# Stick-breaking heads: the causal mask as POOL selects in SBUF in place of a mask matmul into PSUM

## The chip, the cores and the metric

The kernel runs on one core of a Trainium2 chip. The metric is the device time of one execution in microseconds (us). The core's engines are named as the profile names them: PE (TensorE, with PEld for its weight loads), DVE (VectorE), ACT (ScalarE), POOL (GpSimd) and SP (which only issues DMAs here). Each engine takes its own instructions strictly in the order in which they stand in its queue; semaphores tie the engines together.

## What is computed

One decoder layer on 512 tokens of width 2048: a joint input projection, two groups of attention heads side by side, an output projection, a SwiGLU feed-forward part and a last RMSNorm, all in float32. The change touches the first group alone, 16 heads of causal stick-breaking attention with 64 dimensions each. Cut to what matters:

```python
z = jnp.einsum('bqhd,bkhd->bhqk', qf[:, q0:kend], kf[:, :kend])
causal = s < t
log_beta = jax.nn.log_sigmoid(z)
log_one_minus = jnp.where(causal, jax.nn.log_sigmoid(-z), 0.0)
survive = lax.cumsum(log_one_minus, axis=3, reverse=True) - log_one_minus
weights = jnp.where(causal, jnp.exp(log_beta + survive), 0.0)
outs.append(jnp.einsum('bhqk,bkhd->bqhd', weights, vf[:, :kend]))
```

So a key s counts for a query t only where s < t, in two places: in the sum of the logarithms and in the weights.

## The kernel before, in words

Float32 products are made of three passes over operands that are split into a high part (fp32r) and the rest: high by high, high by low, low by high. The long matrix products (input projection, output projection, feed-forward) keep PE fed throughout, and the attention is woven into them.

The stick-breaking part works on blocks. Head h has four key blocks i of 128 keys, taken in the order 3, 2, 1, 0. Scores are held with keys on the partitions and queries on the columns, so block i needs the queries from i*128 on: 128, 256, 384 and 512 columns for i = 3, 2, 1, 0. The 128 columns at the left of a block are its diagonal square, the only place where the mask cuts. There are 64 blocks in all. In what follows **A** is a head of odd number and **B** the even one behind it, and A2 is block 2 of head A. Before (line numbers of the profile) a block runs through these steps:

- scores (`sb_qk`): two matmuls on PE (L600, L601) into a PSUM bank z, then the mask matmul (L602): identity times a bf16 tile that holds -1e30 where the mask cuts, added to the diagonal square of z;
- softplus (`sb_log`, `sb_sp`): ACT takes abs, exp and ln (L614, L615, L616), DVE makes max(z, 0) + that (L623, tile e), ACT copies it to fp32r (L624, tile h) and DVE takes the rest (`sb_lo`, L629, tile l). At masked places z is about -1e30, so softplus is 0;
- running sums over blocks (`sb_acc`) for i = 2 and 1 on POOL: L641 to L651, ten instructions in a head, of which the five of i = 1 (L641, L642, L649, L651, L650) follow each other closely;
- sum (`sb_sum`): two or four matmuls onto z (L661 to L664) that subtract the sums of softplus;
- weights (`sb_w`, `sb_wsplit`): ACT takes exp of z (L669, tile e again; 0 at masked places), DVE casts it (L674) and takes the rest (L675);
- values (`sb_av`): two matmuls (L684, L685) into the head's output bank; behind block 0 ACT and DVE add its two halves (L511, L513), and behind each pair of heads the squares are added up by ACT and POOL (L520, L521).

The loop over the 64 blocks works on several blocks at a time: the logarithms of block j, the sum and weights of j-1, the values of j-2. Between these it pulls steps of the input projection (L390 to L392, with L219 on ACT and L220 on DVE splitting their weights), so that PE has other work while the chain goes over ACT, DVE and POOL. Every second head also gets the q and k of two later heads staged (L488, L491, L497 to L500, L506, L507). The queue order of each engine is not the order of the code: a scheduler sets it when the program is built, except for instructions that are pinned to program order, which are none of those in the list above.

In the constants at the start, DVE makes `identb` and `maskb` and POOL sets and selects `scm`.

Of the kernel before, what the change touches and what calls it, by code (L numbers as in the profile page):

```python
# [8 lines left out]
F32 = mybir.dt.float32  # L9
F32R = mybir.dt.float32r  # L10
BF16 = mybir.dt.bfloat16
I32 = mybir.dt.int32
AF = mybir.ActivationFunctionType
ALU = mybir.AluOpType
AX = mybir.AxisListType

P = 128
# [8 lines left out]
IN_COLS = 4608  # L26
C_SBQ, C_SBK, C_SBV, C_SWQ, C_SWK, C_SWV = 0, 1024, 2048, 3072, 4096, 4352
EPS = 1e-5
NEG = -1.0e30
FAR = 1.0e32  # L30
QSCALE = HD ** -0.5
GF = 4
# [5 lines left out]
def tile_hymba(ctx: ExitStack, tc: tile.TileContext, x, ln_mix, w_in, sb_norm, swa_norm,  # L38
# [6 lines left out]
    const = ctx.enter_context(tc.tile_pool(name="const", bufs=1))  # L45
# [29 lines left out]
    def pz():  # L75
        return zs[1].tile([P, 512], F32, tag="z", name="z", bufs=4)
# [17 lines left out]
    def tmp(dt=F32, name="t"):  # L94
        return phase[1].tile([P, 512], dt, tag="t", name=name, bufs=phase[2])
# [9 lines left out]
    mm = nc.tensor.matmul  # L105
    V = nc.vector
    A = nc.scalar
    G = nc.gpsimd
# [15 lines left out]
    ident = const.tile([P, P], F32, name="ident")  # L124
    make_identity(nc, ident)
    ones = const.tile([P, P], F32, name="ones")
    G.memset(ones, 1.0)
    identb = const.tile([P, P], BF16, name="identb")
    neg1 = const.tile([P, P], F32R, name="neg1")
    negu = const.tile([P, P], F32R, name="negu")  # L130
    maskb = const.tile([P, P], BF16, name="maskb")
    sink = const.tile([P, 16], F32, name="sink")

    def constants():
        V.tensor_copy(out=identb, in_=ident)
        V.tensor_scalar(out=neg1, in0=ones, scalar1=-1.0, scalar2=None, op0=ALU.mult)
        scr = tmp(F32, "scr")[:, 0:P]
        G.affine_select(out=scr, in_=ones, pattern=[[-1, P]], compare_op=ALU.is_ge, fill=0.0,
                        base=0, channel_multiplier=1)
        V.tensor_scalar(out=negu, in0=scr, scalar1=-1.0, scalar2=None, op0=ALU.mult)  # L140
        scm = tmp(F32, "scm")[:, 0:P]
        G.memset(scm, 0.0)
        G.affine_select(out=scm, in_=scm, pattern=[[1, P]], compare_op=ALU.is_gt, fill=NEG,
                        base=0, channel_multiplier=-1)
        V.tensor_copy(out=maskb, in_=scm)
        nc.gpsimd.dma_start(out=sink, in_=sinks[0].partition_broadcast(P))

    gcol = const.tile([P, 48], F32, name="gcol")
# [330 lines left out]
    for c in (3, 4):  # L479
        while pos[0] < c - 3 or pos[1] < 3:  # L480
            step()
        load_x(c)
    turn2 = gain_cols([ln_ffn[0], sb_norm[0], swa_norm[0]], 16)
    defer(8, constants)
    defer(16, turn2)

# [101 lines left out]
    def geom(i):  # L588
        c0 = i * P if i < 3 else 256
        return S - i * P, c0, i * P - c0, S - c0  # L590

    def sb_qk(h, i):
        H = heads[h]
        n, c0, off, W = geom(i)
        B = Head()
        H.blk[i] = B
        zb = pz()
        B.zb, B.z = zb, zb[:, off:W]
        kb = H.ks[:, i * P:(i + 1) * P]
        mm(zb[:, 0:W], lhsT=kb, rhs=H.q1[:, c0:S], start=True, stop=False)  # L600
        mm(zb[:, 0:W], lhsT=kb, rhs=H.q2[:, c0:S], start=False, stop=True)  # L601
        mm(zb[:, off:off + P], lhsT=identb, rhs=maskb, start=False, stop=True, skip_group_check=True)  # L602

    def sb_log(h, i):
        H = heads[h]
# [12 lines left out]
    def sb_sp(h, i):  # L618
        H = heads[h]
        B = H.blk[i]  # L620
        n, c0, off, W = geom(i)
        e = B.e
        V.scalar_tensor_tensor(out=e, in0=B.z, scalar=0.0, in1=e, op0=ALU.max, op1=ALU.add)  # L623
        A.activation(out=B.h[:, off:W], in_=e, func=AF.Copy)  # L624
    def sb_lo(h, i):
        H = heads[h]
        B = H.blk[i]
        n, c0, off, W = geom(i)
        V.tensor_tensor(out=B.l[:, off:W], in0=B.e, in1=f(B.h)[:, off:W], op=ALU.subtract)  # L629
        if i == 3:  # L630
            H.acc[2] = (B.h, B.l, 256)
# [34 lines left out]
    def sb_w(h, i):  # L666
        B = heads[h].blk[i]
        n, c0, off, W = geom(i)
        A.activation(out=B.e, in_=B.z, func=AF.Exp)  # L669

    def sb_wsplit(h, i):
        B = heads[h].blk[i]
        n, c0, off, W = geom(i)
        V.tensor_copy(out=B.wh[:, off:W], in_=B.e)  # L674
        V.tensor_tensor(out=B.wl[:, off:W], in0=B.e, in1=f(B.wh)[:, off:W], op=ALU.subtract)  # L675
# [24 lines left out]
    sb_begin(0)  # L700
    pull(4000.0, sb_mark)
    at(sb_qk, 0)
    for j in range(NJ + 2):
        if j + 3 < NJ and jobs[j + 3][1] == 3:
            sb_begin(jobs[j + 3][0])
        at(sb_log, j)
        at(sb_qk, j + 1)
        pull(SBFILL / 3, sb_mark)
        at(sb_sum, j - 1)
        at(sb_w, j - 1)  # L710
        at(sb_sp, j)
        at(sb_acc, j)
        pull(SBFILL / 3, sb_mark)
        at(sb_av, j - 2)
        at(sb_wsplit, j - 1)
        at(sb_lo, j)
        pull(SBFILL / 3, sb_mark)
# [10 lines left out]
                    base=P, channel_multiplier=1)  # L728
    G.affine_select(out=dist, in_=dist, pattern=[[1, 256]], compare_op=ALU.is_ge, fill=FAR,
                    base=-1, channel_multiplier=-1)  # L730
# [929 lines left out]
```

## Time and profile before

| what | value |
|---|---|
| time, median of 3 runs | 2018.02 us (2017.5 to 2018.03) |
| span of the profiled execution, first to last instruction | 2015.3 us |
| median run less that span | 2.7 us |
| stick-breaking part, first to last mask matmul | 129.1 to 382.5 us |
| granted TensorE clock, mean | 0.998 |

The span is what the trace covers; the time of a run has a little on top of it, for what lies ahead of the first instruction and behind the last. That the granted clock is at 0.998 means that PE's speed was not reduced at any point that matters here. A row of the groups view reads: line, engine, operation, output tile <- input tiles, output size <- input size, count | busy us, mean ns of one | idle time of the engine just before, and who ended it. A row of the timeline reads: start us, duration us, engine, line, operation.

### The profile page before, as it was taken

What the parts mean: (1) busy time and instruction counts of PE and PEld (TensorE: products, weight loads), DVE (VectorE), ACT (ScalarE), POOL (GpSimd) and SP (SyncE); (2) the same over time, 40 slices, a digit from 0 to 9 for tenths busy, and PEclk for the clock granted to TensorE, in tenths of its full rate; (3) what the DMA queues carried; (4) which work ended last, traced back from release to release, by engine and by line L of the source; (5) the groups of instructions that cost most, each with busy time, mean ns of one, the idle gap of its engine ahead of it and who ended that gap; (6) DMA issues with size and microseconds to landing.
All of it is one profiled execution on the core that took longest, in us unless ns stands there. A gap on an engine that the chain in (4) does not pass through costs nothing.

```text
span 2015.3 us, 29246 instructions
## 1 busy us (share of the span) xinstructions
PE 2002.2 (99%) x10412; PEld 1707.3 (85%) x10412; DVE 1453.2 (72%) x1968; ACT 1455.7 (72%) x2009; POOL 1031.9 (51%) x562
## 2 busy tenths in 40 slices
PE   9999999999999999999999999999999999999998
PEld 8888888898788888888888888888888888888886
DVE  4358888768963777777777777777777867767767
ACT  5347777657842477777777777777777788788787
POOL 0014444300100066766667666666766778878883
PEclk9999999999999999999999999999999999999999
DMA  5332222222343354453544535444454743533523
GB/s 192 92 93 65 64 66 71 63 84 67 103 147 114 120 157 125 111 141 101 136 116 120 137 101 140 112 124 132 104 141 106 266 157 111 180 128 106 175 86 115
DMA packets 286369, 240.23 MB, mean 119 GB/s; under 512 B 11024, under 2 KB 237392, under 8 KB 283792
## 3 DMA queue, kind: packets, MB, share of 16 engines
q1 hardware_dynamic: 285552, 235.71, 39.6%
q8 instruction: 82, 1.34, 0.3%
q0 software_dynamic: 288, 1.32, 0.2%
q10 hardware_dynamic: 384, 1.34, 0.2%
q14 instruction: 63, 0.52, 0.1%
HBM read 218.40 MB, written 19.92 MB: 118 GB/s over the span
## 4 chain that ended last, share of the span: by engine, by line
PE 97%; DVE 1%; ACT 1%; issue 0%; DVEq 0%; POOL 0%; ACTq 0%; POOLq 0%
PE o L118 34%; PE m L118 28%; PE m L390 4%; PE m L391 4%; PE m L392 4%; PE m L359 2%; PE m L358 2%; PE m L360 2%; PE o L360 2%; PE o L359 2%; PE o L358 2%; PE z L118 1%; PE z L359 1%; PE z L360 1%; PE z L358 1%; PE z L853 1%
## 5 line engine op out<-in xcount | busy, mean ns | idle before, releaser
L118 POOL TENSOR_TENSOR t<-raw,t 128x1024 f32<-128x1024 f32 x107 | 272.6, 2548 | 277.5 <-ACT hp L118 263.3
L118 DVE TENSOR_TENSOR wlo<-t,hp 128x1024 fp32r<-128x1024 f32 x235 | 286.5, 1219 | 172.3 <-PE o L118 107.5
L118 ACT ACTIVATE whi<-t 128x1024 fp32r<-128x1024 f32 x235 | 249.3, 1061 | 123.1 <-PE o L118 74.7
L118 PE MATMUL o<-hca,whi 128*128 128x512 f32 x880 | 307.5, 391 | 0.0
L118 POOL TENSOR_TENSOR t<-raw,raw 128x1024 f32<-128x1024 f32 x106 | 275.3, 2601 | 16.0 <-issue 10.3
L118 DVE TENSOR_TENSOR wlo<-raw,hp 128x1024 fp32r<-128x1024 f32 x175 | 213.6, 1221 | 81.3 <-issue 50.5
L118 ACT ACTIVATE whi<-raw 128x1024 fp32r<-128x1024 f32 (+1 forms) x177 | 187.1, 1057 | 99.8 <-PE m L118 72.0
L118 PE MATMUL o<-hca,wlo 128*128 128x256 f32 x880 | 244.0, 280 | 0.0
L118 ACT ACTIVATE hp<-t 128x1024 fp32r<-128x1024 f32 x235 | 236.9, 1008 | 0.0
L220 DVE TENSOR_TENSOR wlo<-raw,whi 128x1024 fp32r<-128x1024 f32 x103 | 126.5, 1228 | 137.7 <-ACT whi L219 135.0
L219 ACT ACTIVATE whi<-raw 128x1024 fp32r<-128x1024 f32 x103 | 108.7, 1056 | 152.2 <-PE o L360 75.4
L118 PEld LDWEIGHTS o<-hca,whi 128*128 128x128 f32 x880 | 164.2, 187 | 35.8
L118 PE MATMUL m<-hca,whi 128*128 128x512 f32 x528 | 186.3, 392 | 1.1 <-DVE hca L118 1.1
L118 ACT ACTIVATE hp<-raw 128x1024 fp32r<-128x1024 f32 x179 | 180.8, 1010 | 3.1 <-DVE wlo L118 2.2
L118 PEld LDWEIGHTS o<-hca,wlo 128*128 128x128 f32 x880 | 165.6, 189 | 0.4
L390 PE MATMUL m<-hhi,whi 128*128 128x512 f32 x384 | 156.3, 407 | 0.0
L391 PE MATMUL m<-hlo,whi 128*128 128x512 f32 x384 | 150.5, 392 | 0.0
L392 PE MATMUL m<-hhi,wlo 128*128 128x512 f32 x384 | 150.4, 392 | 0.0
L118 PE MATMUL m<-whi,dca 128*128 128x512 f32 x592 | 146.9, 389 | 0.0
L118 PE MATMUL o<-whi,dca 128*128 128x512 f32 x592 | 146.8, 389 | 0.0
L118 PE MATMUL m<-hca,wlo 128*128 128x256 f32 x528 | 146.3, 280 | 0.0
L118 PEld LDWEIGHTS o<-whi,dca 128*128 128x128 f32 x592 | 111.1, 188 | 23.1
(351 smaller groups left out, 5143.6 us busy)
## 6 DMA issues: line engine op xcount, KB each, us to landing
raw<-in_w_gate_up_dram SPq DMA_DIRECT2D x348, 256.0 KB, 5.2
raw<-in_w_down_dram SPq DMA_DIRECT2D x68, 512.0 KB, 4.8
raw<-in_w_in_dram SPq DMA_DIRECT2D x39, 512.0 KB, 3.5
raw<-in_w_in_dram SPq DMA_DIRECT2D x66, 256.0 KB, 3.3
raw<-in_w_out_dram SPq DMA_DIRECT2D x32, 512.0 KB, 3.8
aT<-w SPq DMA_DIRECT2D x44, 256.0 KB, 3.5
xd<-aT SPq DMA_DIRECT2D x10, 1024.0 KB, 7.1
rx<-in_w_down_dram SPq DMA_DIRECT2D x20, 512.0 KB, 5.7
```

What stands on the lines that cost most here:

```text
L118: return lambda *a, **k: tc.keep_in_program_order(fn(*a, **k))
L219: A.activation(out=hi, in_=raw, func=AF.Copy)
L220: V.tensor_tensor(out=lo, in0=raw, in1=f(hi), op=ALU.subtract)
L358: mm(o, lhsT=lh[:, sl], rhs=hi[:, j, :], start=first, stop=False, skip_group_check=halves)
L359: mm(o, lhsT=lh[:, sl], rhs=lo[:, j, :], start=False, stop=False, skip_group_check=halves)
L360: mm(o, lhsT=ll[:, sl], rhs=hi[:, j, :], start=False, stop=(k == nslab * a - 1), skip_group_check=halves)
L390: mm(o, lhsT=wh, rhs=xh, start=(k == 0), stop=False)
L391: mm(o, lhsT=wh, rhs=xl, start=False, stop=False)
L392: mm(o, lhsT=wl, rhs=xh, start=False, stop=(k == KT - 1))
L853: nc.tensor.transpose(out=pb[:, hh * P:(hh + 1) * P], in_=B.s[hh // 2][:, hh % 2, j * P:(j + 1) * P], identity=ident)
```

## The change

The mask matmul goes, with the tiles `identb` and `maskb` and the instructions that made them. In its place POOL runs an affine select on the diagonal square of tile e, in place, which writes 0 where the mask cuts: once behind the softplus (L623) and once behind the exp of the weights (L669). In the changed file the select is L595, and the lines behind the constants have other numbers: L617 is L623 of before, L624 is L629, L670 is L674, L671 is L675, L504 is L513, L211 is L220, L489, L490, L491 and L498 are L498, L499, L500 and L507, and on POOL L636, L637, L644, L646, L645 and L512 are L641, L642, L649, L651, L650 and L521.

```diff
-    identb = const.tile([P, P], BF16, name="identb")
-    maskb = const.tile([P, P], BF16, name="maskb")
...
-        V.tensor_copy(out=identb, in_=ident)
...
-        G.memset(scm, 0.0)
-        G.affine_select(out=scm, in_=scm, pattern=[[1, P]], compare_op=ALU.is_gt, fill=NEG,
-                        base=0, channel_multiplier=-1)
-        V.tensor_copy(out=maskb, in_=scm)
...
         mm(zb[:, 0:W], lhsT=kb, rhs=H.q2[:, c0:S], start=False, stop=True)
-        mm(zb[:, off:off + P], lhsT=identb, rhs=maskb, start=False, stop=True, skip_group_check=True)
+
+    def causal(e):
+        G.affine_select(out=e[:, 0:P], in_=e[:, 0:P], pattern=[[1, P]], compare_op=ALU.is_gt, fill=0.0,
+                        base=0, channel_multiplier=-1)
...
         V.scalar_tensor_tensor(out=e, in0=B.z, scalar=0.0, in1=e, op0=ALU.max, op1=ALU.add)
+        causal(e)
         A.activation(out=B.h[:, off:W], in_=e, func=AF.Copy)
...
         A.activation(out=B.e, in_=B.z, func=AF.Exp)
+        causal(B.e)
```

PE's queue stays as it was but for the missing mask matmuls and one step of the first head. The queues of DVE, ACT and POOL are put in another order by the scheduler. The names in the rows below carry the tile's number: e2 is the tile of a block 2, and so on.

POOL before, from the running sums of head 4 (a B) to the squares of the heads 2 and 3:

```order
L642 CAST ah2_1830<-e2_1809 128x128
L646 COPY af_1834<-e2_1809 128x128
L641 TENSOR_TENSOR ah2_1830<-e3_1771,e2_1809 128x128
L645 TENSOR_TENSOR af_1834<-e3_1771,e2_1809 128x128
L647 TENSOR_TENSOR al2_1831<-af_1834,ah2_1830 128x256
L641 TENSOR_TENSOR ah1_1885<-af_1834,e1_1862 128x256
L642 CAST ah1_1885<-e1_1862 128x128
L649 TENSOR_TENSOR af_1834<-af_1834,e1_1862 128x256
L651 TENSOR_TENSOR al1_1886<-e1_1862,ah1_1885 128x128
L650 TENSOR_TENSOR al1_1886<-af_1834,ah1_1885 128x256
L521 TENSOR_TENSOR sqA_811<-sqA_811,oc_1846 128x512
```

Nothing of POOL's stands between the running sums of one head and those of the next but these squares.

POOL with the change, first at the seam between head 3 (A, tiles e1_1691 and e0_1734) and head 4 (B, tiles e3_1776 and e2_1815):

```order
L595 AFFINE_SELECT e1_1691<-e1_1691 128x128
L595 AFFINE_SELECT e3_1776<-e3_1776 128x128
L595 AFFINE_SELECT e2_1815<-e2_1815 128x128
L637 CAST ah2_1837<-e2_1815 128x128
L595 AFFINE_SELECT e0_1734<-e0_1734 128x128
L641 COPY af_1841<-e2_1815 128x128
L595 AFFINE_SELECT e3_1776<-e3_1776 128x128
```

Five selects have come in here: the weights' select of A0 stands behind the softplus select and the cast of B2, and the copy and the weights' select of B3 behind it. Then, still on POOL, from the softplus of block 1 of head 4 on:

```order
L595 AFFINE_SELECT e1_1869<-e1_1869 128x128
L636 TENSOR_TENSOR ah1_1893<-af_1841,e1_1869 128x256
L637 CAST ah1_1893<-e1_1869 128x128
L644 TENSOR_TENSOR af_1841<-af_1841,e1_1869 128x256
L646 TENSOR_TENSOR al1_1894<-e1_1869,ah1_1893 128x128
L645 TENSOR_TENSOR al1_1894<-af_1841,ah1_1893 128x256
L512 TENSOR_TENSOR sqA_802<-sqA_802,oc_1853 128x512
L595 AFFINE_SELECT e2_1815<-e2_1815 128x128
L595 AFFINE_SELECT e0_1912<-e0_1912 128x128
```

The first select on a tile e is that of the softplus, the second that of the weights. The weights' select of block 2 stands behind the five running sums of block 1 and the squares, and the softplus select of block 0 behind that.

DVE before, from the softplus of block 1 of head 3 (A) to the rest of its block 0:

```order
L623 SCALAR_TENSOR_TENSOR e1_1688<-z_1641,e1_1688 128x384
L513 TENSOR_TENSOR oA_272<-o_1539,oc_1679 64x512
L629 TENSOR_TENSOR l1_1690<-e1_1688,h1_1689 128x384
L498 CAST q1_1800<-qk_1290 64x512
L499 TENSOR_TENSOR q2_1801<-qk_1290,q1_1800 64x512
L507 TENSOR_TENSOR ks_1802<-qk_1290,ks_1802 64x512
L674 CAST h2_1636<-e2_1635 128x256
L500 CAST q2_1801<-q2_1801 64x512
L675 TENSOR_TENSOR l2_1637<-e2_1635,h2_1636 128x256
L623 SCALAR_TENSOR_TENSOR e0_1730<-z_1694,e0_1730 128x512
L220 TENSOR_TENSOR wlo_1762<-raw_1667,whi_1761 128x1024
L629 TENSOR_TENSOR l0_1732<-e0_1730,h0_1731 128x512
```

Here the casts and rests wait for ACT alone. The same place of DVE's queue with the change:

```order
L617 SCALAR_TENSOR_TENSOR e1_1691<-z_1643,e1_1691 128x384
L504 TENSOR_TENSOR oA_270<-o_1539,oc_1682 64x512
L489 CAST q1_1806<-qk_1283 64x512
L624 TENSOR_TENSOR l1_1693<-e1_1691,h1_1692 128x384
L490 TENSOR_TENSOR q2_1807<-qk_1283,q1_1806 64x512
L491 CAST q2_1807<-q2_1807 64x512
L670 CAST h2_1638<-e2_1637 128x256
L671 TENSOR_TENSOR l2_1639<-e2_1637,h2_1638 128x256
L617 SCALAR_TENSOR_TENSOR e0_1734<-z_1697,e0_1734 128x512
L498 TENSOR_TENSOR ks_1808<-qk_1283,ks_1808 64x512
L211 TENSOR_TENSOR wlo_1767<-raw_1670,whi_1766 128x1024
L624 TENSOR_TENSOR l0_1736<-e0_1734,h0_1735 128x512
```

The cast of the weights of block 2 (L670) now needs POOL's select instead of ACT's exp, and the staging of k has moved from ahead of it to behind the softplus of block 0.

DVE with the change from the softplus of B3 (e3_1776) to that of B1:

```order
L617 SCALAR_TENSOR_TENSOR e3_1776<-z_1740,e3_1776 128x128
L671 TENSOR_TENSOR l1_1693<-e1_1691,h1_1692 128x384
L624 TENSOR_TENSOR sl3_796<-e3_1776,sh3_794 128x128
L617 SCALAR_TENSOR_TENSOR e2_1815<-z_1780,e2_1815 128x256
L670 CAST h0_1735<-e0_1734 128x512
L624 TENSOR_TENSOR l2_1817<-e2_1815,h2_1816 128x256
L671 TENSOR_TENSOR l0_1736<-e0_1734,h0_1735 128x512
L211 TENSOR_TENSOR wlo_1863<-raw_1763,whi_1862 128x1024
L670 CAST wh3_798<-e3_1776 128x128
L617 SCALAR_TENSOR_TENSOR e1_1869<-z_1821,e1_1869 128x384
```

This stretch stands as it did before; the cast L670 and the rests L624 in it now wait for selects.

More of the change, by code (lines that the diff above doesn't have):

```diff
@@ L28 @@
 EPS = 1e-5
-NEG = -1.0e30
 FAR = 1.0e32
@@ L140, in constants @@
         V.tensor_scalar(out=negu, in0=scr, scalar1=-1.0, scalar2=None, op0=ALU.mult)
-        scm = tmp(F32, "scm")[:, 0:P]
-        G.memset(scm, 0.0)
-        G.affine_select(out=scm, in_=scm, pattern=[[1, P]], compare_op=ALU.is_gt, fill=NEG,
-                        base=0, channel_multiplier=-1)
-        V.tensor_copy(out=maskb, in_=scm)
         nc.gpsimd.dma_start(out=sink, in_=sinks[0].partition_broadcast(P))
```

## The prediction

> **What bounds the kernel now.** I read the page first: busy time by engine and the chain that ended last.
>
> ```profile
> span 2015.3 us, 29246 instructions
> PE 2002.2 (99%) x10412; PEld 1707.3 (85%) x10412; DVE 1453.2 (72%) x1968; ACT 1455.7 (72%) x2009; POOL 1031.9 (51%) x562
> PE 97%; DVE 1%; ACT 1%; issue 0%; DVEq 0%; POOL 0%; ACTq 0%; POOLq 0%
> ```
>
> PE works for 2002 of 2015 us and carries 97% of the chain, so a matmul less is time less, as long as PE is not made to wait. The reader should not stop at the averages: POOL at 51% says nothing of the stick-breaking part, where the change lies. So I read the windows there (busy us of PE, PEld, DVE, ACT, POOL) and the mask matmul's own rows.
>
> ```profile
> 226.00:258.00 32.00, 32.00 (x162) 26.44 (x162) 27.84 (x48) 24.69 (x51) 14.97 (x21) 1.00 0.23 67
> L602 PE MATMUL z<-maskb,identb x64: 229/229/230, 129.1 to 382.5; 128*128 128x128 bf16 x64
> ```
>
> PE is full, but DVE is at 27.84 of 32.00, 87%. The 64 masks start 129.1 to 382.5 us, that is 63 steps in 253.4 us, or 32.2 us for a pair of heads (8 blocks). In this time DVE works for 0.87 x 32.2 = 28.0 us and idles for 4.2. That idle time is the room for new waits.
>
> **What the change removes.** The 229 ns of a mask matmul are not its cost, since matmuls overlap. The timeline of PE around one mask tells it by starts:
>
> ```profile
> 220.57 0.39 PE L601 MATMUL z<-q,ks 128*128 128x512 f32 x1
> 220.80 0.23 PE L602 MATMUL z<-maskb,identb 128*128 128x128 bf16 x1
> 220.84 0.48 PE L390 MATMUL m<-hhi,whi 128*128 128x512 f32 x1
> 221.15 0.39 PE L391 MATMUL m<-hlo,whi 128*128 128x512 f32 x1
> 221.38 0.39 PE L392 MATMUL m<-hhi,wlo 128*128 128x512 f32 x1
> ```
>
> A 512-column matmul takes 0.23 us from start to start (221.15 to 221.38). From L601 to L391 there are two of them, 0.46 us, but 0.58 passed: the mask costs 0.12 to 0.13 us, and 64 of them 8 us. (The Trainium skill, "TensorE: Matmul & The Clock Gate", section "Back-to-back issue gap", gives about 81 ns for a 128-column matmul in a stream, which would make 5 us of it, an estimate from that page; the trace's starts say more, and the sum goes by them.) The two DVE casts and two POOL instructions at the start lie beside PE's first loads; I price them at nothing.
>
> **What it adds.** 128 selects on POOL, two in each block, each ahead of something that waits. The rows that price one and the work around it on POOL, then on ACT, then on DVE (mean ns behind the bar and the comma):
>
> ```profile
> L138 POOL TENSOR_SCALAR_AFFINE_SELECT scr<-ones 128x128 f32<-128x128 f32 x1 | 0.3, 304 | 0.0
> L642 POOL CAST ah<-e 128x128 fp32r<-128x128 f32 x32 | 17.1, 534 | 165.9 <-DVE e L623 165.9
> L646 POOL COPY af<-e 128x128 f32<-128x128 f32 x16 | 10.2, 635 | 0.0
> L641 POOL TENSOR_TENSOR ah<-af,e 128x256 fp32r<-128x256 f32 x16 | 11.9, 741 | 4.9 <-DVE e L623 4.9
> L649 POOL TENSOR_TENSOR af<-af,e 128x256 f32<-128x256 f32 x16 | 13.2, 826 | 0.0
> L651 POOL TENSOR_TENSOR al<-e,ah 128x128 fp32r<-128x128 f32 x16 | 10.6, 663 | 0.0
> L650 POOL TENSOR_TENSOR al<-af,ah 128x256 fp32r<-128x256 f32 x16 | 14.5, 907 | 0.0
> L521 POOL TENSOR_TENSOR sqA<-sqA,oc 128x512 f32<-128x512 f32 x6 | 8.0, 1336 | 0.0
> L624 ACT ACTIVATE sh<-e 128x128 fp32r<-128x128 f32 x16 | 5.0, 310 | 10.7 <-DVE e L623 10.7
> L614 ACT ACTIVATE e<-z 128x256 f32<-128x256 f32 x16 | 6.0, 375 | 2.1 <-PE z L602 1.6
> L615 ACT ACTIVATE e<-e 128x256 f32<-128x256 f32 x16 | 6.7, 417 | 0.5
> L616 ACT ACTIVATE e<-e,ones 128x256 f32<-128x256 f32 x16 | 8.2, 510 | 0.5
> L624 ACT ACTIVATE h<-e 128x384 fp32r<-128x384 f32 x16 | 8.4, 525 | 10.3 <-DVE e L623 10.2
> L614 ACT ACTIVATE e<-z 128x512 f32<-128x512 f32 x16 | 9.6, 599 | 1.1 <-PE z L602 0.7
> L520 ACT ACTIVATE oc<-oA 128x512 f32<-128x512 f32 x6 | 3.7, 624 | 0.0
> L615 ACT ACTIVATE e<-e 128x512 f32<-128x512 f32 x16 | 10.0, 627 | 0.2
> L616 ACT ACTIVATE e<-e,ones 128x512 f32<-128x512 f32 x16 | 11.6, 724 | 0.4
> L513 DVE TENSOR_TENSOR oA<-o,oc 64x512 f32<-64x512 f32 x15 | 10.2, 678 | 0.2
> L498 DVE CAST q<-qk 64x512 fp32r<-64x512 f32 x14 | 5.9, 422 | 0.4
> L629 DVE TENSOR_TENSOR l<-e,h 128x384 fp32r<-128x384 f32 x16 | 12.6, 789 | 1.3 <-ACT h L624 1.1
> L499 DVE TENSOR_TENSOR q<-qk,q 64x512 fp32r<-64x512 f32 x14 | 12.6, 902 | 0.6 <-ACT q L497 0.2
> L500 DVE CAST q<-q 64x512 fp32r<-64x512 f32 x14 | 6.3, 454 | 0.5
> L675 DVE TENSOR_TENSOR l<-e,h 128x384 fp32r<-128x384 f32 x15 | 8.2, 548 | 0.3 <-PE z L661 0.2
> L629 DVE TENSOR_TENSOR sl<-e,sh 128x128 fp32r<-128x128 f32 x16 | 4.6, 286 | 0.0
> L675 DVE TENSOR_TENSOR wl<-e,wh 128x128 fp32r<-128x128 f32 x16 | 8.9, 557 | 0.4
> L623 DVE SCALAR_TENSOR_TENSOR e<-z,e 128x512 f32<-128x512 f32 x16 | 11.0, 686 | 6.7 <-ACT e L616 6.7
> ```
>
> One select of this size took 0.304 us at the start, with DVE quiet. POOL's cast of the same size in this part takes 0.534 on average. The select, s, lies between; below nothing it can't go. I take the middle, s = 0.42. In POOL's work 128 of them are 54 us, which fits beside its 15 of 32; the cost is in the queues. Every queue is strict, so DVE, which has most to do, waits wherever the next thing in its queue hangs on a select, and what stands behind it waits too. I walk DVE's queue of the change through a pair of heads, A then B, and count the idle time at each such place: what POOL and ACT need, less what DVE has to do meanwhile.
>
> 1. Cast of A2's weights. From the softplus of A1: a select, five running sums, then the select: s + (0.741 + 0.534 + 0.826 + 0.663 + 0.907 = 3.67) + s. DVE has meanwhile the halves (0.678), L498, L629 of A1, L499, L500: 0.678 + 0.422 + 0.789 + 0.902 + 0.454 = 3.24. Idle 0.43 + 2s. The staging of k, which filled this place, now stands behind it.
> 2. Softplus of B2. From the softplus of B3: s, ACT's copy 0.310, then abs, exp, ln of B2 0.375 + 0.417 + 0.510: 1.61 + s. DVE has 0.548 + 0.286 = 0.83. Idle 0.78 + s.
> 3. Cast of A0's weights, next in DVE's queue. POOL first does the softplus select and the cast of B2: s + 0.534 + s. Idle 0.53 + 2s.
> 4. Softplus of B0. From that of B1: s, copy 0.525, abs 0.599, squares 0.624, exp 0.627, ln 0.724: 3.10 + s. DVE has 0.557 + 0.678 + 0.789 = 2.02. Idle 1.08 + s.
> 5. Cast of B2's weights. POOL, counted from the softplus of B1: s + 3.67 + 1.336 (squares) + s = 5.01 + 2s; DVE is through with the softplus of B0 at 3.10 + s + 0.686. Idle 1.22 + s.
> 6. Cast of B0's weights. Behind the softplus of the next A2 POOL does a select, L642, L646 and the select: 1.17 + 2s, against 0.422 + 0.902 on DVE. Idle 2s - 0.15.
>
> The sum is 3.89 + 9s, or 7.7 us with s = 0.42. Two further places (the softplus of the next A2, the split of the weights behind B0) come to about one select each less overlap; I leave them out, against starts that overlap by some 0.03 us each. DVE's pair then lasts 28.0 + 7.7 = 35.7 us against 32.2 now: 3.5 more. Since the same queue order comes back each pair and each step waits for the one before, this is a loop over DVE, POOL and ACT that PE cannot shorten: PE, which needs 32.2 - 8 x 0.12 = 31.2 us for a pair, waits for the rest. What is late first is a values matmul, since there the slack is smallest:
>
> ```profile
> 226.31 0.43 DVE L675 TENSOR_TENSOR l<-e,h 128x256 fp32r<-128x256 f32 x1
> 226.80 0.37 PE L685 MATMUL o<-l,vst 128*128 128x256 f32 x1
> ```
>
> The rest of A2's weights is ready at 226.74, and PE uses it 0.06 us later. From block 1 of head 1 to that of head 15 there are 7 turns: 7 x 3.5 = 24.5 us. PE's 8 us are inside this, since they only make PE wait longer. Span 2015.3 + 24.5 = 2039.8; with the 2.7 us by which the median run (2018.0) stands above the span, **2042.5 us**.
>
> **Bounds.** Upwards: s = 0.534 gives 3.89 + 4.8 = 8.7, and the two places left out 1.1 more, so 37.8 a pair, 5.6 x 7 = 39: 2057. Downwards: s = 0.304, and running sums that are not held up, as here:
>
> ```profile
> 237.08 0.74 POOL L641 TENSOR_TENSOR ah<-af,e 128x256 fp32r<-128x256 f32 x1
> 239.46 0.74 POOL L650 TENSOR_TENSOR al<-af,ah 128x256 fp32r<-128x256 f32 x1
> ```
>
> Five of them in 3.12 us instead of 3.67, twice a pair: 3.89 + 2.7 - 1.1 = 5.5, 33.5 a pair, 1.3 x 7 = 9: 2027.
>
> **Rivals.**
>
> *The waits are hidden and PE keeps its saving* (the other side). If the loop stays below PE's 31.2 us a pair, PE never waits and the 8 us come off: 2010. For it: DVE's idle time of 4.2 us a pair would be used up first, and 0.304 us is little beside the 4 us of a block. Against it: DVE waits at six places, not one. It decides at new idle time below 3.2 us a pair, while place 5 alone has 1.6. Chance 0.12.
>
> *Waits and saving cancel.* A loop of 32 us, between the low bound and PE's pace: durations on DVE shrink as well when it waits more, by 1.5 us a pair below the low bound. 2014 to 2022. Chance 0.12.
>
> *The selects also hold DVE up.* POOL's cast went from 0.30 (the select's size with DVE quiet) to 0.534 in this part, so the two engines get in each other's way, and each select could hold a DVE instruction for its own length. 16 selects a pair x 0.304 = 4.9 us on DVE's 28.0 if each meets one: the loop becomes 40.6 and the time 7 x 8.4 = 59 above: 2077; half of it, 2060. The Trainium skill, "SBUF — State Buffer", section "SBUF: two separate sides", has it as a rule: DVE with two inputs in SBUF and a POOL instruction take a shared port pair by turns, and the loser waits for the whole instruction. By that rule this rival holds wherever L629 or L675 is met; the 0.534 agrees, but a DVE that waits for selects meets them less. Chance 0.16 for over 2058.
>
> *The forecast*, 2027 to 2058: 0.60.
>
> **How the numbers follow.** Likeliest is 2042.5. The range takes in the bounds and the cancelling case, leaves out the hidden case (0.12) and the end of the port case (0.06): 2014 to 2068. A measurement can tell about 0.2%, 4 us, from no change. Faster by over that: 0.12; within it: 0.12; slower: 0.76.
>
> **What would show it.** In the changed profile: idle time of PE in the stick-breaking part, some 35 us, ended by DVE's L671 and L624 (the rests); DVE's casts L670 waiting for POOL selects; pairs of heads 35 to 36 us apart; about 0.3 to 0.5 us for a select; everything behind that part as long as before. It is wrong if PE is still full there (the hidden case), or if the selects take far longer than the cast of their size, or if DVE's busy time in the part grows by over 10 us (the port case).

## The result, and the profile after

| | before | change |
|---|---|---|
| median, 4 runs each on one chip | 2018.03 us (2017.5 to 2018.18) | 2049.67 us (2048.64 to 2049.74) |
| ratio, with its 95% interval | | 1.0156 [1.0142, 1.0171] |
| span of the profiled execution | 2015.3 us | 2046.9 us |

The change is slower by 31.6 us. First the page of the change: the span, busy time by engine, and the chain that ended last by engine.

```profile
span 2046.9 us, 29202 instructions
PE 2014.3 (98%) x10348; PEld 1707.8 (83%) x10348; DVE 1439.7 (70%) x1966; ACT 1451.9 (71%) x2009; POOL 1074.2 (52%) x688
PE 85%; POOL 6%; ACT 4%; DVE 3%; issue 1%; DVEq 0%; POOLq 0%; ACTq 0%
```

POOL's busy time rose by 42 us and DVE's fell by 13.5, and neither is the news. The chain is: PE went from 97% to 85% of it, and POOL, ACT and DVE have 13%, which before had 2. Where that is, the softplus on DVE tells (one line, 64 times, with the first and last start), before and in the change:

```profile
L623 DVE SCALAR_TENSOR_TENSOR e<-z,e x64: 276/484/693, 130.5 to 386.8; 128x128 f32<-128x128 f32 x16, 128x256 f32<-128x256 f32 x16, 128x384 f32<-128x384 f32 x16, 128x512 f32<-128x512 f32 x16
```

```profile
L617 DVE SCALAR_TENSOR_TENSOR e<-z,e x64: 283/483/693, 133.2 to 417.9; 128x128 f32<-128x128 f32 x16, 128x256 f32<-128x256 f32 x16, 128x384 f32<-128x384 f32 x16, 128x512 f32<-128x512 f32 x16
```

From first to last softplus there are 256.3 us before and 284.7 with the change: 28.4 of the 31.6 us lie in the loop. The first starts 2.7 later, and from the last to the end it is 1628.5 against 1629.0. So the whole loss lies in the stick-breaking part and its start. This stretch of 63 steps is the measure used for every run below. It divides into pairs of heads (8 steps): 32.5 us before, 36.2 with the change. In mid-part, away from start and end, the pairs of the change are 36.8 apart.

What waits for what in that part (engine, tile and line, what released it: us in total, times, longest), before and in the change:

```profile
ACT h L624 <- DVE e L623: 21.9, 32, 1.2
...
ACT sh L624 <- DVE e L623: 10.7, 14, 1.2
```

```profile
ACT h L619 <- POOL e L595: 54.8, 40, 3.1
DVE h L670 <- POOL e L595: 33.9, 45, 3.5
PEld o L680 <- DVE h L670: 21.2, 25, 1.9
ACT sh L619 <- POOL e L595: 19.1, 14, 1.7
...
PEld o L681 <- DVE l L671: 16.9, 34, 1.0
...
PE o L680 <- DVE h L670: 10.8, 17, 1.4
...
PE o L681 <- DVE l L671: 6.8, 15, 0.7
```

Read it from the top: ACT's copy of the softplus waited 33 us for DVE; now it waits 74 us for the select (L595). DVE's cast of the weights (L670) waits 34 us, which it did not before, and PE's values matmuls (L680, L681) wait for that cast and its rest. PE had no such wait before. The selects themselves (the line with its minimum, median and maximum in ns, then its group with busy us and mean ns):

```profile
L595 POOL TENSOR_SCALAR_AFFINE_SELECT e<-e x128: 283/294/935, 133.5 to 422.1; 128x128 f32<-128x128 f32 x128
```

```profile
L595 POOL TENSOR_SCALAR_AFFINE_SELECT e<-e 128x128 f32<-128x128 f32 x128 | 56.2, 442 | 207.3 <-DVE e L617 124.2
```

Half of them take 0.29 us, as at the start of the kernel, and the mean is 0.442.

### The profile page after: what moved, and what is told of

Same layout as the page of the kernel before. It is cut to its first block, busy times and chain, and to the rows that moved or that the text cites. A ratio compares the mean times of both kernels' runs of the same rounds, so it can differ in the third digit from the quotient of the medians.

```text
span 2046.9 us, 29202 instructions
## 1 busy us (share of the span) xinstructions
PE 2014.3 (98%) x10348; PEld 1707.8 (83%) x10348; DVE 1439.7 (70%) x1966; ACT 1451.9 (71%) x2009; POOL 1074.2 (52%) x688
## 3 DMA queue, kind: packets, MB, share of 16 engines
q0 software_dynamic: 288, 1.32, 0.2%
## 4 chain that ended last, share of the span: by engine, by line
PE 85%; POOL 6%; ACT 4%; DVE 3%; issue 1%; DVEq 0%; POOLq 0%; ACTq 0%
PE o L117 34%; PE m L117 28%; PE m L350 2%; PE m L349 2%; PE m L351 2%; POOL e L595 2%; PE m L382 2%; PE m L381 2%; PE o L350 2%; PE o L351 2%; PE m L383 2%; PE o L349 2%; PE z L117 1%; POOL ah L636 1%; PE z L351 1%
## 5 line engine op out<-in xcount | busy, mean ns | idle before, releaser
L211 DVE TENSOR_TENSOR wlo<-raw,whi 128x1024 fp32r<-128x1024 f32 x103 | 128.5, 1247 | 133.9 <-ACT whi L210 130.9
L595 POOL TENSOR_SCALAR_AFFINE_SELECT e<-e 128x128 f32<-128x128 f32 x128 | 56.2, 442 | 207.3 <-DVE e L617 124.2
```

The costliest lines, as they stand in the source:

```text
L211: V.tensor_tensor(out=lo, in0=raw, in1=f(hi), op=ALU.subtract)
L595: G.affine_select(out=e[:, 0:P], in_=e[:, 0:P], pattern=[[1, P]], compare_op=ALU.is_gt, fill=0.0, base=0, channel_multiplier=-1)
```

## The experiments

All times are medians, with the ratio to the kernel before and its 95% interval. The kernel before had 2017.8 us beside the first eight and 2018.1 beside the last four. "Stretch" is the time from first to last softplus. The line numbers are those of the change, except where a kernel's own rows are shown.

| kernel | time, us | ratio | stretch, us |
|---|---|---|---|
| before | 2018.0 | 1 | 256.3 |
| the change | 2049.67 | 1.0156 [1.0142, 1.0171] | 284.7 |
| e1_no_mask | 2013.49 | 0.9979 [0.997, 0.9989] | 250.3 |
| e2_aside | 2020.97 | 1.0015 [1.0006, 1.0024] | 259.1 |
| e3_softplus_only | 2044.14 | 1.013 [1.0115, 1.0145] | 282.6 |
| e4_weights_only | 2028.14 | 1.0051 [1.0036, 1.0066] | 265.9 |
| e5_both_masks | 2058.06 | 1.02 [1.0185, 1.0216] | 295.2 |
| e6_twice | 2085.2 | 1.0334 [1.0316, 1.0351] | 319.1 |
| e7_later_values | 2040.44 | 1.0112 [1.0097, 1.0127] | 279.4 |
| e8_later_sum | 2060.17 | 1.021 [1.0195, 1.0225] | 295.9 |
| e9_dve_softplus | 2046.94 | 1.0144 [1.013, 1.0157] | 283.1 |
| e10_dve_both | 2031.69 | 1.0067 [1.0055, 1.008] | 266.4 |
| e11_dve_softplus_later | 2037.13 | 1.0094 [1.0079, 1.011] | 274.7 |
| e12_sums_ahead | 2055.5 | 1.0185 [1.0171, 1.0199] | 291.3 |

### e1: the mask left out, and e2: the selects without anybody waiting

The theory is that the waits for the selects cost the time. The rival is that the selects, by their mere work on POOL, hold DVE up. e1 takes the selects out of the change; e2 puts as many into the kernel before, whose mask matmul stays, and lets them write into a tile of their own that nobody reads.

```diff
# e1, from the change
-        causal(e)
-        causal(B.e)
# e2, from before
+    def aside(e):
+        G.affine_select(out=sbt(BF16, "aside", P), in_=e[:, 0:P], pattern=[[1, P]], compare_op=ALU.is_gt, fill=0.0,
+                        base=0, channel_multiplier=-1)
...
+        aside(e)
+        aside(B.e)
```

> The mask is left out altogether: neither mask matmul nor selects. All theories expect PE's saving alone: about 8 us below the kernel before (2018), so 2010, with PE never waiting in the stick-breaking part. If it stays at 2018, the mask matmuls were free and the saving of the sum was wrong.

> The kernel before, with mask matmuls, plus the 128 selects on POOL, which read the same squares but write a tile that nobody reads. POOL's work is that of the change; nothing waits for a select but what stands behind it in POOL's queue. Theory of the waits (DVE and ACT stand still because the next thing in their queues hangs on a select): 2016 to 2022, as before. Theory of the load (selects hold DVE up through their work alone): most of the change's 32 us stays, 2035 to 2050.

Without masks the kernel, which then computes something else, takes 2013.5 us. So leaving the matmuls out is worth 4.3 us there, not 8 (why, is told with the prediction below), and no kernel that adds mask work to this one can be expected below 2013.5. As many selects of the same squares cost 3.1 us when nobody reads what they write, and 36.2 us (2049.67 - 2013.49) when somebody does. The 3.1 even hold some waiting: ACT's exp, which overwrites the tile that they read, waits 11 us for them in e2. The work itself, with its contention (a select took 0.523 us on average in e2), is a tenth of the loss. The waits are the rest.

### e3 and e4: one select each; e5: both, with the mask matmul kept

```diff
# from before; e3 has the first call alone, e4 the second, e5 both
+    def causal(e):
+        G.affine_select(out=e[:, 0:P], in_=e[:, 0:P], pattern=[[1, P]], compare_op=ALU.is_gt, fill=0.0,
+                        base=0, channel_multiplier=-1)
...
+        causal(e)
+        causal(B.e)
```

> The kernel before, with mask matmuls, plus only the softplus select in place (it changes no value). Theory of the waits: only places 2 and 4 of the sum (softplus of B2 and of B0) and the two places left out grow, by one select each, about 4 x 0.44 = 1.8 us a pair, part of it within the slack that PE has: 2018 to 2026. Theory of the load: half of the change's loss, about 2034.

> The kernel before, with mask matmuls, plus only the weights' select in place (it changes no value). Theory of the waits: places 1, 3, 5 and 6 (the casts of weights) keep most of their idle time, because there the select also stands behind POOL's other work: 2024 to 2040, clearly more than with the softplus selects alone. Theory of the load: about 2034, the same as with the softplus selects alone.

> The change with the mask matmuls left in (they change no value then). Theory of the waits: PE stands still for some 20 us of the stick-breaking part anyway, so 64 more matmuls fill idle time: 2048 to 2053, against 2049.7 of the change. If PE's work still counted in full, 4 to 8 us more: 2054 to 2058.

The select of the softplus costs 26.3 us, that of the weights 10.3. The two together, less the 4.3 of e1, come to 2017.8 + 36.6 - 4.3 = 2050.1, beside 2049.7 measured. That the sum fits this well is partly luck: e5 has both selects and the matmuls at 2058.1, 3.6 more than the parts add up to, and so in the presence of the selects the 64 mask matmuls are worth 8.4 us. The expectation that they would fill idle time of PE (2048 to 2053) was wrong.

The larger half is that for which I had expected little: 2044.1 lies far above the 2018 to 2026 of the theory of the waits, and the 2028.1 of the weights' selects is below it, where it was expected above. The waits in e3 (line numbers of that kernel: L605 the select, L629 ACT's copy, L634 DVE's rest):

```profile
ACT h L629 <- POOL e L605: 55.0, 40, 2.6
...
DVE l L634 <- ACT h L629: 24.5, 37, 1.1
```

The softplus select stands in the middle of a row DVE, POOL, ACT, DVE: softplus, select, copy, rest. Behind ACT's copy stand the logarithms of the next block in ACT's queue, so a late select delays the next softplus as well. The weights' select has only DVE's cast behind it. That this is why the softplus select costs more is read from the queues; no run shows it by itself.

### e6: every select twice

```diff
# from the change
         causal(e)
+        causal(e)
...
         causal(B.e)
+        causal(B.e)
```

> The change with each select issued twice in a row (the second changes nothing). Theory of the waits: the sum counts 9 to 11 selects one behind the other in a pair of heads; another 0.3 us in each is 2.7 to 3.3 us a pair and 19 to 23 us over 7 turns: 2068 to 2074. Theory that a first wait costs and its length doesn't (a fixed handover): below 2058. Theory of the load: 128 x 0.3 us more of POOL's work takes as much from DVE, up to 38 us: over 2080.

The second 128 selects cost 35.5 us, that is 0.278 us each. The first 128 cost 36.2 (against e1), 0.283 us each. A select takes 0.29 where it is not disturbed, and 0.442 on average in the change. So the time grows as though all 16 selects of a pair stood one behind the other at their undisturbed length, or some ten of them at their average one. The forecast's sum, 3.89 + 9s, had nine count. That 2085 lies in the range of the theory of the load is not for its reason: DVE's busy time did not grow but fell, from 1439.7 to 1434.5 us. How many selects are joined up is shown by the chain of waits in one pair of the change (265.7 to 302.6 us, by line):

```profile
by line: POOL e L595 17.7%; issue 8.6%; DVE e L617 5.4%; POOL ah L636 5.2%; ACT whi L210 5.1%; POOL af L644 4.9%; POOL al L645 4.2%; ACT e L608 4.2%; POOL al L642 4.0%; DVE h L670 4.0%; POOL al L646 3.5%; ACT e L609 3.4%; POOL sqA L512 3.4%
```

Fourteen of the sixteen selects stand on this chain, with 17.7% of it or 6.5 us; only two are hidden. The selects and the running sums (L636 to L646) and squares (L512), all on POOL, have over 40% of the chain between them, though POOL as a whole is busy half of the time. The path that sets the pair runs through most of POOL's queue.

### e7 and e8: the work that waits put one block later

```diff
# from the change; both
-    for j in range(NJ + 2):
+    for j in range(NJ + 3):
...
-        at(sb_av, j - 2)
-        at(sb_wsplit, j - 1)
+        at(sb_av, j - 3)
+        at(sb_wsplit, j - 2)
# e8 only
-        at(sb_sum, j - 1)
-        at(sb_w, j - 1)
+        at(sb_sum, j - 2)
+        at(sb_w, j - 2)
```

> The change with the weights' cast and rest and the values' matmuls of a block moved one block later in the code (two and three blocks behind instead of one and two), so that the weights' selects have a block's time. Theory of the waits: the idle time at the casts (about 3.9 of 10.5 us a pair) goes, that behind the softplus selects stays, as with the softplus selects alone (2044): 2036 to 2045. Theory of the scheduler's order (the new order of the queues costs, not the selects): any value, but no tie to 2044.

> As the run before it, and the sums and the exp of the weights also one block later, so that the rests behind the softplus have a block's time too. Theory of the waits: PE no longer waits for rests at once, but ACT's copy still stands behind the softplus select and holds up ACT's next logarithms, so half of the softplus part stays at most: 2020 to 2036. If ACT's hold-up is what costs in the softplus part: 2040 or more, as in the run before.

More distance between the weights' select and its users (e7) takes 9.2 us off. PE's values no longer wait. What is late now is the sum, which waits for the rest of the softplus: `PE z L659 <- DVE l L624` and the same of PEld have 25 us. More distance there too (e8) makes it worse, not better:

```profile
PEld z L591 <- ACT e L664: 32.1, 42, 2.1
PE z L591 <- ACT e L664: 14.4, 18, 1.6
```

The scores of a new block (L591) now wait for ACT's exponential (L664) of an old one. The scores, the sum and the exponential of a block use one PSUM bank z, and there are four of these banks, so a bank is held a block longer; the distance is paid for with banks. It is paid for with tiles too: ACT's abs (L608) waits 18 us for the rest of the weights (L671) of the old block whose tile e it takes over. e8 changes one thing in what is computed: the running sum of block 2 takes block 3's softplus, where before and the change take what stands in that tile later, its weights.

### e9, e10 and e11: the mask by DVE

A DVE multiply by a tile of ones and zeros needs no handover to POOL.

```diff
# from the change
+    keep = const.tile([P, P], F32, name="keep")
...
+        G.affine_select(out=keep, in_=ones, pattern=[[1, P]], compare_op=ALU.is_gt, fill=0.0,
+                        base=0, channel_multiplier=-1)
...
-        causal(e)
+        V.tensor_tensor(out=e[:, 0:P], in0=e[:, 0:P], in1=keep, op=ALU.mult)
# e10 also
-        causal(B.e)
+        V.tensor_tensor(out=B.e[:, 0:P], in0=B.e[:, 0:P], in1=keep, op=ALU.mult)
# e11: e9, and the later values of e7
```

> The change, but the mask of the softplus is a DVE multiply of the first 128 columns by a tile of ones and zeros, right behind the softplus on DVE; the weights keep their POOL select. Theory handover (ACT's copy waits for a trip to POOL, and stands behind POOL's running sums there): 8 trips a pair go, 8 multiplies of about 0.29 us (the size of the 128x128 rest on DVE) come on DVE, 2.3 us; the weights alone cost 10 us in the run before, so 2026 to 2036, pairs 33.7 to 35 us apart, and ACT's h copy waits for DVE no longer than before the change. Theory DVE is the bound (its work is what counts, and each us more on it is a us more a pair): 36.8 + 2.3 a pair, 2060 or more. Theory that any mask on the way from softplus to copy costs the same wherever it is done: 2044 to 2052.

> The change with both masks as DVE multiplies, none on POOL: 16 multiplies of about 0.29 us a pair, 4.6 us more work on DVE. If DVE keeps the 4.2 us of idle time that it has a pair with the mask matmul: 28.0 + 4.6 + 4.2 = 36.8 a pair, no better than the change, about 2050. If what costs is the trip to POOL and DVE's idle time can be filled: 33.5 to 35.5 a pair, 2025 to 2040.

> The DVE mask of the softplus together with the weights' split and the values matmuls one block later (which alone took 9 us off the change). If the two gains lie in different places: 2018 to 2029. If they are the same slack: as the better of the two alone.

e9 is a miss: 2046.9, only 2.7 us better than the change, though in e4 the weights' select alone had cost 10. It lies in the range of the third theory, that a mask on the way from softplus to copy costs the same wherever it is done. In the pair from 264.9 us on DVE's idle time fell from 10.5 to 6.8 us, and its busy time rose from 26.4 to 30.1. The largest piece of the idle time that is left, 2.90 us, stands at one place, shown here in the timelines of POOL and DVE (start, us, what; in brackets the idle time ahead and what ended it; in this kernel L598 is the select, L620 the softplus, L621 the multiply):

```profile
286.69 1.29 POOL L515 TENSOR_TENSOR sqA<-sqA,oc 128x512 f32<-128x512 f32 x1
287.94 0.54 POOL L598 TENSOR_SCALAR_AFFINE_SELECT e<-e 128x128 f32<-128x128 f32 x2
...
284.81 0.56 DVE L627 TENSOR_TENSOR l<-e,h 128x384 fp32r<-128x384 f32 x1 [0.59 <-ACT h L622]
288.27 0.36 DVE L673 CAST h<-e 128x256 fp32r<-128x256 f32 x1 [2.90 <-POOL e L598]
...
289.07 0.68 DVE L620 SCALAR_TENSOR_TENSOR e<-z,e 128x512 f32<-128x512 f32 x1
...
293.60 0.41 DVE L620 SCALAR_TENSOR_TENSOR e<-z,e 128x256 f32<-128x256 f32 x1
...
296.78 0.29 DVE L621 TENSOR_TENSOR e<-e,keep 128x128 f32<-128x128 f32 x1
```

DVE waits 2.90 us for the weights' select of B2, which stands on POOL behind the running sums and the squares, and the softplus of B0 stands behind it in DVE's queue. In the change that softplus stands ahead of the cast; DVE waited 1.86 us for it and then 0.95 at the cast, 2.81 in all. So nothing was won here: one wait was taken away, and the other, behind the same queue on POOL, is as much longer. The last two rows show a second reason: the scheduler did not put the multiply right behind its softplus, but 3.2 us behind it in the case of block 2, so ACT's copy waits for DVE again (48.5 us for h, from 21.9 before).

With the weights' mask on DVE too (e10) the last handover to POOL goes, and the time falls by 15.3 us to 2031.7. That is 18 us above e1 for all 128 masks, less than the 26.3 of the softplus selects alone, which speaks against the third theory. DVE then has little idle time left:

```profile
129.00:399.00 270.00, 256.05 (x1243) 213.27 (x1242) 244.19 (x495) 197.84 (x401) 102.08 (x165) 1.00 0.22 65
```

It is busy (third of the five busy times) for 244 of 270 us, 90%, against 84% before (217 of 259, shown below). e11 adds e7's later values to e9 and gains 9.8 us, as much as in e7; its 2018 to 2029 had counted on a larger gain of e9. So e7's gain lies in another place than e9's, while e9's own is small in both. None of the three beats the kernel before.

### e12: the running sums out of the way of one select

```diff
# from the change
-        at(sb_sum, j - 1)
-        at(sb_w, j - 1)
         at(sb_sp, j)
         at(sb_acc, j)
+        at(sb_sum, j - 1)
+        at(sb_w, j - 1)
```

> The change with the running sums of a block written ahead of the weights of the block before, so that on POOL the sums of block 2 (L636 to L642) stand ahead of the weights' select of block 3 and no longer between it and the softplus select of block 1; ACT's queue is the same as in the change, DVE's nearly. It changes one thing in what is computed: the running sum of block 2 takes block 3's softplus, where before and the change take what stands in that tile later, its weights. Theory queue (place 4 is 1.15 us longer than forecast because the softplus select of block 1 stands behind these sums, 1.9 us of POOL work, which themselves wait for ACT's exponential of block 3): DVE's idle time at place 4 falls from 2.65 to 1.5 to 1.9 us, pairs 35.6 to 36.2 us apart, 2040 to 2046. Theory sum of POOL's work (all that POOL does in a pair counts, wherever it stands): 2048 to 2052, with the idle time of DVE at other places instead.

The place concerned, in the change first: POOL, then ACT, then DVE.

```profile
281.21 0.92 POOL L595 TENSOR_SCALAR_AFFINE_SELECT e<-e 128x128 f32<-128x128 f32 x1 [1.59 <-ACT e L664]
282.21 0.49 POOL L636 TENSOR_TENSOR ah<-e,e 128x128 fp32r<-128x128 f32 x1
282.67 0.46 POOL L640 TENSOR_TENSOR af<-e,e 128x128 f32<-128x128 f32 x1
283.21 0.74 POOL L642 TENSOR_TENSOR al<-af,ah 128x256 fp32r<-128x256 f32 x1
283.90 0.29 POOL L595 TENSOR_SCALAR_AFFINE_SELECT e<-e 128x128 f32<-128x128 f32 x1
...
284.22 0.53 ACT L619 ACTIVATE h<-e 128x384 fp32r<-128x384 f32 x1 [1.83 <-POOL e L595]
...
280.76 1.22 DVE L211 TENSOR_TENSOR wlo<-raw,whi 128x1024 fp32r<-128x1024 f32 x1
...
282.31 0.55 DVE L617 SCALAR_TENSOR_TENSOR e<-z,e 128x384 f32<-128x384 f32 x1
...
284.78 0.56 DVE L624 TENSOR_TENSOR l<-e,h 128x384 fp32r<-128x384 f32 x1 [0.79 <-ACT h L619]
287.20 0.69 DVE L617 SCALAR_TENSOR_TENSOR e<-z,e 128x512 f32<-128x512 f32 x1 [1.86 <-ACT e L610]
```

The softplus of B1 ends at 282.86, and its select starts at 283.90, behind three running sums of B2, which themselves began only after the weights' select of B3. In e12 these sums stand ahead of that weights' select:

```profile
284.57 0.79 POOL L642 TENSOR_TENSOR al<-af,ah 128x256 fp32r<-128x256 f32 x1
285.31 0.74 POOL L595 TENSOR_SCALAR_AFFINE_SELECT e<-e 128x128 f32<-128x128 f32 x1
287.80 0.29 POOL L595 TENSOR_SCALAR_AFFINE_SELECT e<-e 128x128 f32<-128x128 f32 x1 [1.75 <-DVE e L617]
...
284.69 1.21 DVE L671 TENSOR_TENSOR l<-e,h 128x512 fp32r<-128x512 f32 x1
...
287.19 0.54 DVE L617 SCALAR_TENSOR_TENSOR e<-z,e 128x384 f32<-128x384 f32 x1
...
288.68 0.56 DVE L624 TENSOR_TENSOR l<-e,h 128x384 fp32r<-128x384 f32 x1
291.09 0.69 DVE L617 SCALAR_TENSOR_TENSOR e<-z,e 128x512 f32<-128x512 f32 x1 [1.86 <-ACT e L610]
```

At the place itself it came as expected: the select follows its softplus at once, the idle 0.79 ahead of the rest is gone, and from the softplus of B1 to that of B0 it takes 3.90 us instead of 4.89. But the time is 2055.5, 5.8 more than the change. The idle time ahead of the casts of the two blocks 0 (places 3 and 6) rose from 1.05 and 0.67 to 1.36 and 1.90, and a rest of 512 columns that takes 0.69 elsewhere took 1.21 beside the sums. So the place is rightly explained, and the gain there is lost again at the next ones. My range of 2040 to 2046 took one queue's gain for the loop's; the rival, that POOL's work counts wherever it stands, comes nearer, and even its 2052 was too little.

## The prediction, point by point

**The forecast, waits at six places, was right in its main mechanism, and in size within its range**: 2042.5 forecast, 2049.7 measured, inside the case's own 2027 to 2058. Its terms:

- *The mask matmuls, 8 us.* The price holds: without selects (e1) the stretch is 6.0 us shorter, and PE stands idle for 1.7 us of it (busy 248.6 of 250.3), waiting for the rests of weights. That only 4.3 us are left of it in the time is because the first softplus starts 2.2 us later in e1 (132.7 against 130.5 us), as in the change. With the selects they are worth 8.4 (e5 against the change). I had them inside the waits, worth nothing. That step was wrong: "a loop over DVE, POOL and ACT that PE cannot shorten". The values, the scores and the sums on PE are part of the loop, as I read it, and what PE does less shortens it. The order of DVE's queue differs between e5 and the change as well; how much of the 8.4 is that was not separated.
- *The select, 0.42 us.* Measured 0.442 on average.
- *DVE's work, 28.0 us a pair.* Measured 26.4 in the pair from 265.7 us on. The rests got shorter: L629 of 128x384 took 789 ns before (in the prediction's rows), and of L675's 128x256 there is this row of before, beside those of the change:

```profile
L675 DVE TENSOR_TENSOR l<-e,h 128x256 fp32r<-128x256 f32 x16 | 11.8, 740 | 1.0
```

```profile
L624 DVE TENSOR_TENSOR l<-e,h 128x384 fp32r<-128x384 f32 x16 | 8.9, 559 | 8.0 <-ACT h L619 7.8
...
L671 DVE TENSOR_TENSOR l<-e,h 128x256 fp32r<-128x256 f32 x16 | 6.8, 425 | 1.5
```

- *DVE's idle time, 7.7 us.* Measured 10.5 in that pair, by place, from DVE's timeline there:

| place | forecast, us | measured, us |
|---|---|---|
| 1 cast of A2's weights | 1.27 | 1.16 |
| 2 softplus of B2 | 1.20 | 1.50 |
| 3 cast of A0's weights | 1.37 | 1.05 |
| 4 softplus of B0 | 1.50 | 2.65 |
| 5 cast of B2's weights | 1.64 | 0.95 |
| 6 cast of B0's weights | 0.69 | 0.67 |
| left out: weight split behind B0, next A2 | 0 | 1.32 |
| small waits, under 0.2 each, and gaps | 0 | 1.2 |

Four of the six places are within 0.35 us. **Place 4 was mis-sized**: "from that of B1: s, copy, ..." counted the select as if it followed its softplus at once, but on POOL it stood behind the running sums of block 2. e12, which takes the sums away from there, shows it: 1.86 us are left. What place 4 took, place 5 gave back in part. And the two places that I left out as "about one select each less overlap" have 1.32 us.

- *The pair, 35.7 us, and 7 turns.* 26.4 + 10.5 = 36.9; measured 36.8. The work was put 1.6 too high and the idle time 2.8 too low, so that the pair is only 1.2 out is partly luck. Over the whole stretch the loop lost 28.4 us instead of 24.5, and 2.7 more were lost at its start, which I hadn't looked at. The rows, of before and of the change:

```profile
130.54 0.29 DVE L623 SCALAR_TENSOR_TENSOR e<-z,e 128x128 f32<-128x128 f32 x1 [1.90 <-ACT e L616]
131.49 1.23 DVE L220 TENSOR_TENSOR wlo<-raw,whi 128x1024 fp32r<-128x1024 f32 x1 [0.66 <-ACT whi L219]
```

```profile
132.03 1.23 DVE L211 TENSOR_TENSOR wlo<-raw,whi 128x1024 fp32r<-128x1024 f32 x1 [2.56 <-ACT whi L210]
133.18 0.28 DVE L617 SCALAR_TENSOR_TENSOR e<-z,e 128x128 f32<-128x128 f32 x1
```

With the mask matmul gone from the program, the scheduler put a weight split ahead of the first softplus instead of behind it. All kernels here without that matmul have their first softplus at 132.7 us or later, those with it at 131.7 or earlier.

- *Where PE waits.* Forecast some 35 us of idle time in the part, ended by L671 and L624; PE idles 18 us of the part (290.00 less 272.01 in the row below), and what it waits for are the casts and rests of the weights, L670 and L671. The rests of the softplus (L624) come up with 1.5 us here, and to 25 only in e7, once the values have more room. That the loss is larger than PE's idle time is no contradiction: PE is shown busy for 272 us with 1254 matmuls, where before 1308 took 259, so waits between overlapping matmuls count as busy.

**The port rival, that selects hold DVE up, had the wrong direction.** Busy time of the part (PE, PEld, DVE, ACT, POOL), before and in the change:

```profile
129.00:388.00 259.00, 259.00 (x1308) 214.72 (x1308) 217.29 (x372) 197.61 (x402) 114.83 (x166) 1.00 0.23 67
```

```profile
129.00:419.00 290.00, 272.01 (x1254) 216.06 (x1253) 203.66 (x373) 193.43 (x401) 157.14 (x292) 0.99 0.20 60
```

DVE's work fell by 14 us for the same instructions. A DVE that waits for POOL's selects runs less beside POOL, as I read it, and e2 prices the work of 128 selects, contention included, at 3.1 us. It is the select that is held up: the one at 281.21 above took 0.92, and ended 0.15 us behind the weight split on DVE that it met (280.76 + 1.22 = 281.98). It is no single case: of the 108 selects that the timeline of the change shows singly, 54 took over 0.35 us, and every one of them began beside a DVE instruction and ended 0.14 to 0.16 us behind it. That agrees with the rule of the Trainium skill, "SBUF — State Buffer", section "SBUF: two separate sides", that of the two the one that started first has the port for its whole instruction; the case is the one in which POOL came second.

**The hidden case and the cancelling case** both needed a loop near PE's pace. e1 shows how little room there was: with no mask at all the kernel gains 4.3 us.

## What to carry to other kernels

A PE instruction of 0.1 us on a full PE can be cheaper than a "free" one on an engine that is half idle, if the latter stands between two other engines in a loop: here each of 128 selects cost 0.28 us on average, nearly all of its undisturbed length. Price a handover by what stands ahead of it in its engine's queue, and expect the waits that it makes to be slack of one loop: what was gained at one place was lost at the next (e12), or one wait took over the other's length (e9). And a version without the work at all (e1) tells first how much there is to win.

## What the runs showed of the hardware

The clock that PE was granted fell for short times in this part. Two windows of 10 us in the change, and then two pairs of heads, one of which holds such a window (behind the busy times the granted clock):

```profile
230.00:240.00 10.00, 8.44 (x34) 6.71 (x33) 7.87 (x15) 7.16 (x15) 5.97 (x9) 0.83 0.16 47
270.00:280.00 10.00, 8.57 (x33) 7.05 (x34) 6.23 (x14) 6.74 (x16) 3.83 (x9) 0.83 0.19 54
...
265.70:302.60 36.90, 34.31 (x156) 27.60 (x155) 26.41 (x50) 24.70 (x51) 20.47 (x38) 0.95 0.20 59
302.60:339.40 36.80, 33.89 (x158) 26.52 (x157) 26.31 (x50) 24.70 (x51) 20.42 (x38) 1.00 0.20 57
```

In both short windows PE was busy for some 85% and got 0.83 of its clock on average. Cut into windows of 1 us, the clock is not 0.83 anywhere for long: it is 0.50 for some 3.4 us (in full from 236 to 238 us and from 273 to 276) and 1.00 ahead of that and behind it. Shortly ahead of it, each time, PE stood idle for 1.42 us (from 233.07 and from 269.87 us). The pair with the reduced clock lasts 36.9 us, the next one with the full clock 36.8, so this cost next to nothing here; at half the clock for twice 3.4 us PE can have lost some 3.4 of the 31.6 us at most, an estimate from these rows. Why the clock fell there and not behind other idle times as long (1.41 us from 196.91) stays open.
